# Sums of weights of four recurrent pairs formed in DRAM by adding DMAs on GpSimd's queue

## The chip, the cores and the metric

The kernel runs on one core of one Trainium2 chip. The core has five engines with a queue of instructions each: TensorE (PE in the profile, with its weight loads as PEld), VectorE (DVE), ScalarE (ACT), GpSimd (POOL) and SyncE (SP, which here only issues DMAs). Each engine takes its instructions in the order in which they were written into its queue; a semaphore that an instruction waits for holds up everything behind it on the same engine. The metric is the device time of one execution in microseconds.

## What is computed

One layer of a decoder: a normalised input goes through a combined projection into dilated attention heads and gated recurrent heads, then through an output projection and a gated convolution mixer. Only the recurrent part of the projection is touched by the change. Cut to that:

```python
u = rms_norm(h, norm1_g[layer])                       # h: 1024 tokens x 1024
proj = u @ w_in[layer]
aq, ak, av, hq, hf, hi, hg = jnp.split(proj, IN_SPLITS, axis=-1)
...
rec = hgrn2_mixer(hq.reshape(B, S, HGRN_HEADS, HGRN_FDIM),
                  hf.reshape(B, S, HGRN_HEADS, HGRN_FDIM),
                  hi.reshape(B, S, HGRN_HEADS, HGRN_IDIM), lb)
rec = rms_norm(rec, hgrn_norm_g[layer].reshape(HGRN_HEADS, HGRN_IDIM))
rec = rec * jax.nn.silu(hg.astype(jnp.float32).reshape(B, S, HGRN_HEADS, HGRN_IDIM))
```

`hq`, `hf` and `hg` have four heads of 128 columns each, so twelve blocks of weights, 1024 x 128.

## The kernel before

**Products.** Every float32 product is made of three TensorE products of rounded parts: an operand is split into a high part (`hi`, a copy in a narrower format, made on ACT, line 88) and the rest (`lo`, a subtraction on DVE, line 90). Lines 492 to 494 are those three products, 128x128 by 128x512 each.

**Seven products for eight.** Two blocks of weights are taken as a pair, whose four quarters of 128x512 are called a11, a12 (first block) and a21, a22 (second block). The pair is multiplied with the input by a Strassen-like scheme with seven products (`pair_block`). It needs, beside the four quarters, four sums: s1 = a21+a22, s3 = a21+a11, s2 = s1+a11, s4 = a12+s2. Class `PairMix` loads the four quarters into five staging buffers (`raww`) and makes the sums in place on DVE, one addition of 128x512 each (lines 164 to 166 and 183).

**The ring.** `Ring` holds a plan, a list of all weight tiles in the order in which they are used. For each it takes a staging buffer, has SP load 256 KB into it (line 68, or 300 and 155 for other layouts), splits it, and keeps five splits ahead of TensorE. A staging buffer is loaded anew when the subtraction on line 90 has read the tile that was in it.

**Order in time.** First come two passes over the input in eight steps each: the attention's values (`V`, written to DRAM tensor `vd`) and the recurrence's values (`I`, written to `ivd`). During `V`, the squares of the input are summed for the first norm: ACT squares a piece (line 444), POOL adds it to `sums0` or `sums1`, one for each half of the tokens (line 446). Between `V` and `I`, `rms1` multiplies these sums with a column of ones on TensorE (tile `sst`, line 452), and ACT and DVE make the tokens' scales from it. After that come the attention's projections (`qk`), the attention with one recurrent pair beside it (`HG[0]`), then four more pairs (`HG[1]` to `HG[4]`, the subject of the change) with the recurrence woven in (`dense`, `hg_block`), the last pair without the scheme, the output projection, and the mixer.

**What sets the order.** TensorE's order is the order of the program text. On the other engines a scheduler places instructions by its own estimate of when their inputs are there; only what is passed through `pin` keeps the order of the text. The squares' sums on POOL are pinned among themselves. Tiles in DRAM come from the pool `drv`.

**On POOL** there is little: the fourteen sums of squares until 47 us, then, from 77 us on, fills and scalings for the attention's mask (`far_t`, `tri`, `vec`, `sel`, lines 666 to 676) and later one scaling for each attention score tile (line 718).

The lines around which the seam between `V` and `I` turns:

```python
    ring.step = 1
    ring.fill(2)
    for hf in range(2):
        square_x(hf, NCT - 1, NCT - 1)
    ...
    rms1()
```

Of the kernel before, what the change touches and what calls it, by code (L numbers as in the profile page):

```python
# [10 lines left out]
F32 = mybir.dt.float32  # L11
# [3 lines left out]
ALU = mybir.AluOpType  # L15
PSUM = bass.MemoryType.PSUM

P = 128
# [3 lines left out]
H2 = 512  # L22
# [228 lines left out]
def hybrid_kernel(ctx: ExitStack, tc: tile.TileContext, xT, w_qk, w_tok, w_hg, w_out, w_up,  # L251
                  w_down, vecs, amask, hmask, out):
    nc = tc.nc
    PE, DVE, ACT, POOL = nc.tensor, nc.vector, nc.scalar, nc.gpsimd
# [32 lines left out]
    plan = []  # L287

    ORDER = ("a11", "s2", "a12", "s3", "s1", "a22", "s4")

    def want_mix(key, a, b, heads):
        m = PairMix(nc, a, b, heads)
        plan.extend(((key, x), getattr(m, x)) for x in ORDER)

    def tok(m, kh, c):

        def load(ring):
# [6 lines left out]
    HG = [(("hf", 0), ("hq", 0)), (("hg", 0), ("hg", 1)), (("hf", 1), ("hq", 1)), (("hf", 2), ("hq", 2)),  # L304
          (("hg", 2), ("hg", 3)), (("hf", 3), ("hq", 3))]
    def w_of(kind, h):
        return w_hg[4 * {"hq": 0, "hf": 1, "hg": 2}[kind] + h]
# [3 lines left out]
    for p in range(4):  # L311
        want_mix(("qk", p), w_qk[2 * p], w_qk[2 * p + 1], True)
    want_mix(HG[0], w_of("hf", 0), w_of("hq", 0), False)
    for pair in HG[1:-1]:
        want_mix(pair, w_of(*pair[0]), w_of(*pair[1]), False)
    plan.extend(((key, x), w_of(*key)[:, x * H2 : (x + 1) * H2]) for key in HG[-1] for x in range(2))

    OUT_BLOCKS = [[(hf, 0, d) for d in range(NCT) for hf in range(2) if d < SHARED or hf == 0], [(0, 1, d) for d in range(NCT)],
# [12 lines left out]
    for f in range(NFF):  # L331
        if f < 2:
            plan += [((x, f), part(f, i)) for x, i in (("a11", 0), ("a12", 3), ("a21", 1), ("a22", 2))]
        else:
            m = Mix(nc, w_up[f])
# [3 lines left out]
    ring = Ring(nc, ringp, plan)  # L339
# [56 lines left out]
    drv = drv_cm.__enter__()  # L396
# [12 lines left out]
    def vtile(name):  # L409
        return at.tile([P, H2], F32, tag="vi", name=name, bufs=4)  # L410
# [50 lines left out]
    def split_sum(x, c, src):  # L461
        hi, lo = (y[:, c] for y in opn[x])
        pin(ACT.copy(hi, src))
        pin(DVE.tensor_sub(lo, src, f32(hi)))

    def sums_a(c):
        x11, x12 = xt[0, c], xt[1, c]
        g = col(V_G1 + c)
        pin(DVE.tensor_sub(x11, x12, x11))
        pin(ACT.mul(x11, x11, g))  # L470
        pin(ACT.mul(x12, x12, g))

    def sums_b(c):

        x11, x21, x12, x22 = xt[0, c], xt[0, KS + c], xt[1, c], xt[1, KS + c]
        g2 = col(V_G1 + KS + c)

        def less(x, src, y):
            pin(DVE.scalar_tensor_tensor(x, src, g2, y, op0=ALU.mult, op1=ALU.subtract))

        split_sum("T1", c, x11)
        less(x12, x22, x12)
        less(x22, x22, x11)
        less(x21, x21, x22)
        split_sum("T2", c, x22)
        split_sum("T3", c, x12)

    def sums_c(c):
        split_sum("T4", c, xt[0, KS + c])
# [49 lines left out]
    def tok_step(key, c, banks, order):  # L539

        w = ring.get((key, c))
        for t in order:
            bh, bl = opn[OPS1[2 * (t // KS) + c // KS]]
            tk = slice((t % KS) * P, (t % KS + 1) * P)
            three(banks[t], (bh[:, c % KS, tk], bl[:, c % KS, tk]), w, c == 0, c == NCT - 1)
        ring.done((key, c))
# [12 lines left out]
    def tok_out(dst, t, x, src):  # L559
        if src is x or t % 2:  # L560
            DVE.tensor_scalar(x, src, R1T[:, t : t + 1], 1.0, op0=ALU.mult, op1=ALU.mult)
        else:
            ACT.mul(x, src, R1T[:, t : t + 1])
        nc.scalar.dma_start(dst[t * P : (t + 1) * P], x)

    fill = Fill()

    ring.order = ring.pin = pin
# [33 lines left out]
    for c in range(NCT):  # L602
        tok_step("I", c, V, range(NCT) if c < 4 else TURN)
        if c < 2:
            sums_a(2 + c)
        if c < 3:
            sums_b(1 + c)
        if c == 0:
            for t in range(NCT):
                tok_out(vd, t, vt[t], vt[t])  # L610
        if 4 <= c:
            sums_c(c - 4)
    ring.order = ring.pin = lambda ins: ins
    ring.step = 99
    for t in TURN:
        x = vtile(f"it{t}")
# [201 lines left out]
    with pool("hg", "right") as hg:  # L818
# [8 lines left out]
        def tile_of(kind, h, hf):  # L827
            tag, bufs = {"hf": ("A", 4), "hq": ("E", 5), "hg": ("GH"[h // 2], 4)}[kind]
            return ht(tag, f"{tag}{h}_{hf}", bufs)
# [108 lines left out]
        for hf in range(2):  # L938
            for kind, h in HG[0]:
                x = tile_of(kind, h, hf)  # L940
# [693 lines left out]
```

## Time and profile before

| | us |
|---|---|
| median of 3 runs | 1147.45 |
| lowest and highest of them | 1146.85, 1148.58 |
| the profiled execution, its time | 1148.54 |
| its span in the trace | 1146.7 |
| TensorE busy | 1133.0 |
| VectorE busy | 959.9 |
| ScalarE busy | 587.0 |
| GpSimd busy | 87.7 |

The 1.8 us between the profiled execution's time and its span lie outside of the first and last traced instruction. Busy time counts an instruction from its start to its modelled end. On TensorE consecutive products overlap: a 128x512 product is listed with 0.39 us, while the next one starts 0.23 us after it; so a short wait of TensorE can hide within its busy time, and starts have to be compared. Line numbers are those of the kernel before; in the changed kernel the same lines stand 7 to 24 further down.

### The profile page before, as it was taken

The numbers are of one execution on the slowest core, as the hardware profiler recorded it, in microseconds if no ns is written. First come the engines' busy times: TensorE is split into PE (matmuls) and PEld (weight loads), VectorE is DVE, ScalarE is ACT, GpSimd is POOL, SyncE is SP. The second block draws the span as 40 slices with busy tenths as digits, with TensorE's granted clock in tenths as the row PEclk, the third lists the DMA queues.
The fourth block names the chain that finished last, engine by engine and source line by source line (L and its number), as shares of the span: only waits on it lengthen the run. The fifth ranks groups of instructions, "written<-read, shape, count | busy, mean of one in ns | idle before, by whom it ended". The sixth has DMA issues, their size and how long they took to land.

```text
span 1146.7 us, 17921 instructions
## 1 busy us (share of the span) xinstructions
PE 1133.0 (99%) x6412; PEld 929.9 (81%) x6412; DVE 959.9 (84%) x1748; ACT 587.0 (51%) x1177; POOL 87.7 (8%) x107
## 2 busy tenths in 40 slices
PE   9999999999999999999999999999999999999996
PEld 7887777778888888878788888888888888888885
DVE  7685877778999975889999989888988789857987
ACT  6444445465788875555434434343434344444553
POOL 5200233330000002000000000000000000000000
PEclk9999999999999999999999999999999999999998
DMA  7135222224313542321233233322332377435532
GB/s 250 49 108 152 57 73 65 85 75 159 110 57 110 169 134 94 92 65 46 70 114 113 89 102 129 111 78 97 128 111 83 116 262 230 118 101 175 156 114 80
DMA packets 98633, 129.84 MB, mean 113 GB/s; under 512 B 25008, under 2 KB 44240, under 8 KB 98544
## 3 DMA queue, kind: packets, MB, share of 16 engines
q1 hardware_dynamic: 84256, 104.03, 29.5%
q10 hardware_dynamic: 14288, 24.67, 5.8%
q8 instruction: 50, 0.82, 0.3%
q14 instruction: 39, 0.32, 0.1%
HBM read 97.58 MB, written 31.09 MB: 112 GB/s over the span
## 4 chain that ended last, share of the span: by engine, by line
PE 91%; DVE 7%; issue 1%; ACT 1%; DMA 1%; ACTq 0%; DVEq 0%; SPq 0%
PE p L1235 11%; PE p L1233 11%; PE p L1234 11%; PE w L492 5%; PE w L494 5%; PE w L493 5%; PE ds L1533 3%; PE ds L1534 3%; PE ds L1532 3%; PE da L1533 2%; PE da L1534 2%; PE da L1532 2%; PE po L492 2%; PE po L494 2%; PE po L493 2%; PE S L705 2%
## 5 line engine op out<-in xcount | busy, mean ns | idle before, releaser
L88 ACT CAST whi<-raww 128x512 fp32r<-128x512 f32 x257 | 157.6, 618 | 219.1 <-PE p L1234 75.2
L90 DVE TENSOR_TENSOR wlo<-raww,whi 128x512 fp32r<-128x512 f32 x258 | 179.9, 699 | 30.5 <-ACT whi L88 28.6
L88 ACT CAST whi<-r 128x512 fp32r<-128x512 f32 x70 | 43.6, 623 | 83.4 <-PE ds L1533 47.8
L90 DVE TENSOR_TENSOR wlo<-r,whi 128x512 fp32r<-128x512 f32 x70 | 48.0, 687 | 19.1 <-ACT whi L88 18.4
L1532 PE MATMUL ds<-fhi,whi 128*128 128x512 f32 x160 | 62.3, 389 | 0.0
L1534 PE MATMUL ds<-fhi,wlo 128*128 128x512 f32 x160 | 62.2, 389 | 0.0
L1233 PE MATMUL p<-b1h,whi 128*128 128x512 f32 x160 | 62.2, 389 | 0.0
L1234 PE MATMUL p<-b1l,whi 128*128 128x512 f32 x160 | 62.2, 389 | 0.0
L1235 PE MATMUL p<-b1h,wlo 128*128 128x512 f32 x160 | 62.2, 389 | 0.0
L1533 PE MATMUL ds<-flo,whi 128*128 128x512 f32 x160 | 62.2, 389 | 0.0
L718 POOL TENSOR_SCALAR P<-P,st 128x128 f32<-128x128 f32 (+7 forms) x64 | 46.4, 731 | 101.8 <-DVE st L717 96.6
L1506 POOL TENSOR_TENSOR facc<-facc,sqf 128x256 f32<-128x256 f32 x2 | 1.5, 736 | 673.8 <-ACT sqf L1505 673.8
L90 DVE TENSOR_TENSOR flo<-rawf,fhi 128x512 fp32r<-128x512 f32 x70 | 48.0, 686 | 3.9 <-ACT fhi L88 3.9
L88 ACT CAST fhi<-rawf 128x512 fp32r<-128x512 f32 x70 | 43.1, 616 | 14.6 <-PE p L1235 5.0
L716 ACT ACTIVATE P<-P,st 128x128 f32<-128x128 f32 (+7 forms) x64 | 35.7, 559 | 27.5 <-DVE st L714 27.5
L1262 ACT ACTIVATE cv<-cv 128x512 f32<-128x512 f32 x44 | 27.8, 633 | 40.3 <-DVE cv L1255 40.3
L1255 DVE SCALAR_TENSOR_TENSOR cv<-g,vec,cv 128x511 f32<-128x511 f32 (+2 forms) x92 | 44.7, 491 | 3.6 <-ACT cv L1252 3.3
L1532 PE MATMUL da<-fhi,whi 128*128 128x512 f32 x120 | 46.7, 389 | 0.0
L1533 PE MATMUL da<-flo,whi 128*128 128x512 f32 x120 | 46.7, 389 | 0.0
L1534 PE MATMUL da<-fhi,wlo 128*128 128x512 f32 x120 | 46.7, 389 | 0.0
L714 DVE CUSTOM_DVE_ANT_0 P<-S,mask 128x128 f32<-128x128 f32 (+7 forms) x64 | 28.9, 487 | 8.7 <-PE S L707 7.5
L1532 PEld LDWEIGHTS ds<-fhi,whi 128*128 128x128 f32 x160 | 30.0, 188 | 6.3
(622 smaller groups left out, 3408.7 us busy)
## 6 DMA issues: line engine op xcount, KB each, us to landing
raww<-in_w_up_dram SPq DMA_DIRECT2D x88, 256.0 KB, 2.9
rawf<-spT SPq DMA_DIRECT2D x40, 256.0 KB, 2.7
r<-in_w_down_dram SPq DMA_DIRECT2D x40, 256.0 KB, 3.3
spB<-a ACTq DMA_DIRECT2D x30, 256.0 KB, 2.2
spT<-t ACTq DMA_DIRECT2D x30, 256.0 KB, 2.1
rawf<-spB SPq DMA_DIRECT2D x30, 256.0 KB, 2.7
raww<-in_w_out_dram SPq DMA_DIRECT2D x28, 256.0 KB, 2.8
raww<-in_w_hg_dram SPq DMA_DIRECT2D x24, 256.0 KB, 2.6
```

The source lines that it names most:

```text
L88: self.pin(self.high(hi[:, :w], raw))
L90: self.pin(low.tensor_sub(lo[:, :w], raw, f32(hi[:, :w])))
L492: PE.matmul(ps, a[0], b[0], start=start, stop=False)
L493: PE.matmul(ps, a[0], b[1], start=False, stop=False)
L494: PE.matmul(ps, a[1], b[0], start=False, stop=stop)
L718: POOL.tensor_scalar(Pt[:, :n], Pt[:, :n], st[:, 3:4], 1.0, op0=ALU.mult, op1=ALU.mult)
L1233: PE.matmul(ps, hi[:, s], bhi, start=(start and n == 0), stop=False)
L1234: PE.matmul(ps, hi[:, s], blo, start=False, stop=False)
L1235: PE.matmul(ps, lo[:, s], bhi, start=False, stop=(stop and n == len(rhs) - 1))
L1532: PE.matmul(ps[d], hi[:, s], ahi, start=(k == 0), stop=False)
L1533: PE.matmul(ps[d], hi[:, s], alo, start=False, stop=False)
L1534: PE.matmul(ps[d], lo[:, s], ahi, start=False, stop=(k == NPAIR - 1))
```

## The change

```diff
+    wsum = {}
+
+    def quad(pair, x):
+        m, i = {"a11": (0, 0), "a12": (0, 1), "a21": (1, 0), "a22": (1, 1)}[x]
+        return w_of(*pair[m])[:, i * H2 : (i + 1) * H2]
+
     for pair in HG[1:-1]:
-        want_mix(pair, w_of(*pair[0]), w_of(*pair[1]), False)
+        plan.extend(((pair, x), quad(pair, x) if x[0] == "a" else lambda ring, pair=pair, x=x: ring.raw(wsum[pair, x]))
+                    for x in ORDER)
...
+    SUMS = (("s1", "a21", "a22"), ("s3", "a21", "a11"), ("s2", "a22", "s3"), ("s4", "a12", "s2"))
+
+    def sum_begin(pair):
+        for x, a, _ in SUMS:
+            wsum[pair, x] = drv.tile([P, H2], F32, name=f"ws{pair[0][0]}{pair[0][1]}_{x}")
+            nc.sync.dma_start(wsum[pair, x], quad(pair, a))
+
+    def sum_add(pair, i):
+        x, _, b = SUMS[i]
+        POOL.dma_start(wsum[pair, x], quad(pair, b) if b[0] == "a" else wsum[pair, b], accum_op=ALU.add, max_dma_last_dim=2048)
...
         if 4 <= c:
             sums_c(c - 4)
+        if c < len(HG) - 2:
+            sum_begin(HG[1 + c])
+        elif c > 4:
+            for i in (0, 1) if c == 5 else (2,) if c == 6 else (3,):
+                for pair in HG[1:-1]:
+                    sum_add(pair, i)
```

For each of the four pairs, four tiles of 128x512 in DRAM (`ws...`) first receive a copy of one quarter, by a DMA on SP's queue, and then a second quarter or an earlier sum, by a DMA on POOL's queue that adds to what is there. s2 waits for s3, and s4 for s2. In the text the copies stand in the steps 0 to 3 of `I`, the additions in its steps 5 to 7; neither is pinned. Later the ring loads all seven tiles of a pair as plain tiles; `PairMix` is left with the attention's pairs and `HG[0]`. So 16 DVE additions go, and 16 copies, 16 adding DMAs and 12 more loads of the ring (28 for 16) come.

TensorE's list of instructions is the same, row for row. On POOL this is the order around the last sums of squares (names: `sq0_6` is the square of piece 6 of the first half of the tokens; `DMASW` are the semaphores of POOL's own DMAs, `DMAHW` those of SP's and ACT's). Before:

```order
L446 TENSOR_TENSOR sums1_233<-sums1_233,sq1_5_442 128x512 [waits Activation_49]
L446 TENSOR_TENSOR sums0_231<-sums0_231,sq0_6_484 128x512 [waits Activation_49]
L446 TENSOR_TENSOR sums1_233<-sums1_233,sq1_6_487 128x512 [waits Activation_49]
L446 TENSOR_TENSOR sums0_231<-sums0_231,sq0_7_514 128x512 [waits Activation_49]
L446 TENSOR_TENSOR sums1_233<-sums1_233,sq1_7_517 128x512 [waits Activation_49]
L673 MEMSET far_t_1112 32x1024 [waits DVE_49,Pool_49]
```

And in the changed kernel, from the first sum of piece 6 to the last of piece 7:

```order
L453 TENSOR_TENSOR sums0_231<-sums0_231,sq0_6_484 128x512 [waits Activation_49]
L453 TENSOR_TENSOR sums1_233<-sums1_233,sq1_6_487 128x512 [waits Activation_49]
L582 DMA wshg0_s2_622<-wshg0_s3_620 128x512 [waits DMAHW6_49,DMASW1_49]
L582 DMA wshf1_s1_668<-in_w_hg_dram 128x512 [waits DMAHW1_49]
L582 DMA wshf1_s3_670<-in_w_hg_dram 128x512 [waits DMAHW2_49]
L582 DMA wshg0_s4_624<-wshg0_s2_622 128x512 [waits DMAHW7_49,DMASW2_49]
L582 DMA wshf1_s2_672<-wshf1_s3_670 128x512 [waits DMAHW3_49,DMASW4_49]
L582 DMA wshf2_s1_715<-in_w_hg_dram 128x512 [waits DMAHW6_49]
L582 DMA wshf2_s3_717<-in_w_hg_dram 128x512 [waits DMAHW7_49,DMASW0_49]
L453 TENSOR_TENSOR sums0_231<-sums0_231,sq0_7_514 128x512 [waits Activation_49]
L582 DMA wshf1_s4_674<-wshf1_s2_672 128x512 [waits DMAHW4_49,DMASW6_49]
L453 TENSOR_TENSOR sums1_233<-sums1_233,sq1_7_517 128x512 [waits Activation_49]
```

Two more additions (s1 and s3 of the pair hg0) stand ahead of piece 6, six behind the last sum and ahead of the fill of `far_t`. So the scheduler has moved ten of the sixteen ahead of the end of the pass `V`, and eight of them stand between the sums of piece 6 and the second sum of piece 7, which TensorE's product on line 452 reads.

On DVE, these rows stand in the first of the four pairs, just after the attention has ended (`G` are that pair's outputs, `w...` the banks of its products, `lb` small vectors of the recurrence, `wlo` the splits of the ring). Before:

```order
L90 TENSOR_TENSOR wlo56_3321<-raww43_2933,whi56_3320 128x512
L164 TENSOR_TENSOR raww49_3384<-raww47_3360,raww48_3362 128x512
L927 TENSOR_TENSOR lb_m_3280<-vec_63 128x4
L165 TENSOR_TENSOR raww47_3360<-raww46_3358,raww47_3360 128x512
L928 TENSOR_TENSOR lb_e_3281<-vec_63,lb_m_3280 128x4
L929 TENSOR_TENSOR lb_e_3281<-vec_63,lb_m_3280 128x4
L522 TENSOR_TENSOR G0_1_3325<-G0_0_3306,w37_3326 128x512
```

In the changed kernel:

```order
L90 TENSOR_TENSOR wlo56_3369<-raww46_3366,whi56_3368 128x512 [waits DMAHW4_49,PE_49,Activation_49]
L951 TENSOR_TENSOR lb_m_3326<-vec_63 128x4
L952 TENSOR_TENSOR lb_e_3327<-vec_63,lb_m_3326 128x4 [waits DVE_49]
L953 TENSOR_TENSOR lb_e_3327<-vec_63,lb_m_3326 128x4
L955 TENSOR_TENSOR lb_m_3326<-lb_e_3327 128x4 [waits Activation_49]
L956 RECIPROCAL lb_m_3326<-lb_m_3326 128x4 [waits DVE_49]
L957 TENSOR_TENSOR lb_67<-lb_e_3327,lb_m_3326 128x4 [waits DVE_49]
```

The two additions in place (`raww` from `raww`) are gone, and the small vectors follow the split at once.

## Prediction

> **What bounds the kernel now.** I read the busy times first, then the waits of the busiest engine, then the two stretches that the change touches.
>
> ```profile
> PE 1133.0 (99%) x6412; PEld 929.9 (81%) x6412; DVE 959.9 (84%) x1748; ACT 587.0 (51%) x1177; POOL 87.7 (8%) x107
> PE warm L420 <- DVE eps L281: 1.1, 1, 1.1
> PE w L492 <- ACT u L520: 1.0, 1, 1.0
> PE w L492 <- DVE G L530: 0.9, 1, 0.9
> PE p0g L1233 <- DVE h L1128: 0.8, 1, 0.8
> PE v L492 <- DVE whi L88: 0.3, 1, 0.3
> PE p L1235 <- DVE wlo L90: 0.2, 1, 0.2
> ```
>
> The first line is the page's: TensorE is busy for 99% of the span. The other six are the whole list of TensorE's waits (total, times, longest): 4.3 us altogether. Its list of instructions is the same in both kernels, so the change can win only from these waits and from waits too short to be listed. And whatever makes TensorE wait longer somewhere is paid in full, since no later wait is long enough to swallow it.
>
> ```profile
> 260.00:285.50 25.50, 24.64 (x162) 20.41 (x161) 21.63 (x45) 15.79 (x31) 0.00 (x0) 1.00 0.55 179
> 285.50:440.00 154.50, 154.50 (x851) 128.50 (x852) 140.49 (x253) 121.37 (x312) 3.97 (x4) 1.00 0.38 115
> ```
>
> These two stretches (start and end, length, then busy time of PE, PEld, DVE, ACT, POOL, granted clock, DMA share, GB/s) hold the four pairs. DVE is at 91% in the second, yet TensorE has no gap there. DVE's load is high but covered: TensorE sets the pace.
>
> **What goes: 16 additions on DVE.**
>
> ```profile
> L165 DVE TENSOR_TENSOR raww<-raww,raww 128x512 f32<-128x512 f32 x4 | 2.9, 726 | 0.0
> L164 DVE TENSOR_TENSOR raww<-raww,raww 128x512 f32<-128x512 f32 x4 | 2.8, 689 | 0.1
> L166 DVE TENSOR_TENSOR raww<-raww,raww 128x512 f32<-128x512 f32 x4 | 2.7, 680 | 0.0
> L183 DVE TENSOR_TENSOR raww<-raww,raww 128x512 f32<-128x512 f32 x4 | 2.7, 680 | 0.0
> 272.23 0.69 DVE L164 TENSOR_TENSOR raww<-raww,raww 128x512 f32<-128x512 f32 x1
> 276.52 0.69 DVE L523 TENSOR_TENSOR G<-w,G 128x512 f32<-128x512 f32 x1 [0.73 <-PE w L494]
> 278.40 0.68 DVE L166 TENSOR_TENSOR raww<-raww,raww 128x512 f32<-128x512 f32 x1
> 284.68 0.68 DVE L530 TENSOR_TENSOR G<-G,w 128x512 f32<-128x512 f32 x1
> 285.50 0.47 PE L492 MATMUL w<-B22h,whi 128*128 128x512 f32 x1 [0.86 <-DVE G L530]
> ```
>
> DVE loses 2.9 + 2.8 + 2.7 + 2.7 = 11.1 us. On TensorE's path only one place counts. At 285.50 it has waited 0.86 us for DVE's evacuation on line 530. DVE was last idle ahead of 276.52, for 0.73 us, and has been busy almost without a gap since. One removed addition lies in that stretch (278.40, 0.68 us); one like that of 272.23 lies ahead of the idle time, which has swallowed it. Without the addition in the stretch the evacuation comes 0.7 us earlier, and since the order there shifts more than one row, I count the whole wait: **0.9 us won** (0.86), with 0 as the other end if the recurrence's work on DVE moves into the place. Behind it nothing else is late: the 154.5 us after it show no gap. Of waits too short to be listed I count nothing in the sum.
>
> **What is added and hidden.** The 16 copies stand on SP between the loads of `I`.
>
> ```profile
> 23.34 1.79 DVE L90 TENSOR_TENSOR wlo<-raww,whi 128x512 fp32r<-128x512 f32 x1
> 28.46 1.77 DVE L90 TENSOR_TENSOR wlo<-raww,whi 128x512 fp32r<-128x512 f32 x1
> 34.08 0.69 DVE L90 TENSOR_TENSOR wlo<-raww,whi 128x512 fp32r<-128x512 f32 x1 [1.91 <-ACT whi L88]
> 3.62 0.44 SPq L431 DMA_DIRECT2D xs_kp<-in_xT_dram  x1
> SPq L300 <- DVE wlo L90: 36.0, 7, 10.4
> 28.70:51.56 22.86, 22.86 (x104) 18.93 (x102) 14.54 (x19) 11.57 (x20) 6.84 (x5) 1.00 0.15 47
> raww<-in_w_hg_dram SPq DMA_DIRECT2D x24, 256.0 KB, 2.6
> spT<-t ACTq DMA_DIRECT2D x30, 256.0 KB, 2.1
> x<-in_xT_dram SPq DMA_DIRECT2D x8, 256.0 KB, 5.6
> ```
>
> SP issues a DMA in 0.44 us, so 16 copies take 7 us of SP. SP has 36.0 us in which it waits for a staging buffer in seven of these loads, each released by a subtraction (the first three rows, which end at 25.13, 30.23 and 34.77 us). The copies of one pair follow each release. The DMA engines are 15% busy then. No copy from DRAM to DRAM is in this trace; its landing lies between a store's 2.1 us and the 5.6 us of the loads in the crowded first microseconds. Even with 5.6 us the four copies of the second pair have landed at 30.23 + 4 x 0.44 + 5.6 = 37.6 us, before POOL asks for them (38.97, below). So copies cost nothing; were the cover gone, a late weight tile would hold TensorE by up to one landing, 5.6 us at most. The 12 more loads of the ring (12 x 2.6 = 31 us if none overlapped another) come where the DMA engines are used for 0.55 and 0.38 of the time (the two stretches above), and a staging buffer that no longer holds a quarter for three sums comes free sooner; were that cover gone, each late tile would cost up to 2.6 us. What they read has landed long before.
>
> **What is added and not hidden.** It is POOL's queue at the end of the pass `V`.
>
> ```profile
> 35.89 3.08 POOL L446 TENSOR_TENSOR sums<-sums,sq 128x512 f32<-128x512 f32 x2 [6.20 <-ACT sq L444]
> 44.70 2.77 POOL L446 TENSOR_TENSOR sums<-sums,sq 128x512 f32<-128x512 f32 x2 [5.73 <-ACT sq L444]
> 77.18 0.95 POOL L673 MEMSET far_t<- 32x1024 f32 x1 [29.71 <-DVE T4l L464]
> 44.00 1.15 ACT L444 ACTIVATE sq<-x 128x512 f32<-128x512 f32 x2
> 51.40 1.84 PE L452 MATMUL sst<-ones,sums 128*128 128x1 f32 x16
> L446 POOL TENSOR_TENSOR sums<-sums,sq x14: 1286/1740/1752, 13.0 to 46.2; 128x512 f32<-128x512 f32 x14
> ```
>
> Now the last two sums end at 44.70 + 2.77 = 47.47 us, and TensorE needs them at 51.40: slack 3.9 us. In the changed kernel seven adding DMAs stand ahead of the first of these two sums and one more between them, after the sums of piece 6, which end at 35.89 + 3.08 = 38.97 us (the two DMAs ahead of these fall into POOL's 6.2 idle microseconds). Let c be how long one such DMA holds POOL, and w the time from there to its landing. From 38.97: three DMAs are issued (3c). The fourth, hg0_s4, waits for the landing of the first and runs within the next wait: the fifth, hf1_s2, adds hf1_s3, which was issued third, so it begins at 3c + w and ends at 4c + w. Two more (6c + w), one sum (1.39 us, half of 2.77), hf1_s4 (its input landed at 4c + 2w, earlier for w below 2c + 1.39), the last sum (1.39): the sums are ready at **38.97 + 7c + w + 2.78**.
>
> The trace has no DMA on this queue, so both are bounded by rows. c: from SP's issue, 0.44 us, to POOL's own pass over a tile of this size, median 1.74 us. w: from a store's 2.1 us less 0.4 of issue, 1.7 us, to 5.6 less 0.4, 5.2 us. With the low ends the formula gives 46.5, less than the 45.15 + 2.78 = 47.9 at which the squares (ACT's row at 44.00) let the sums be ready, and TensorE doesn't wait. With the high ends hf1_s4 is held by its input (4c + 2w = 17.4), and the end is 38.97 + 17.4 + 1.74 + 1.39 = 59.5: a wait of 8.1 us. I take c = 1.4, as a loop of POOL's program over 128 rows, nearest to its fastest passes (2.77 / 2), and w = 2.6, as a load of the same size: 38.97 + 9.8 + 2.6 + 2.78 = 54.15, a **wait of 2.75 us** at 51.40. All that TensorE has behind it (the steps of `I`) moves with it, and DVE's and ACT's scales with that.
>
> The Trainium skill (DMA: Bandwidth & Descriptors, section "Anatomy of one DMA — SWDGE (gpsimd) path") fits a DMA of this queue with 2.0 us plus its bytes at 436 GB/s, from issue to semaphore, 2.6 us for 256 KB. By it, and with c as taken, w would be 1.2 us, the wait 1.35 us and the result 1147.9 us, an estimate from that page; no run here shows such a DMA yet, and the fit is for plain loads, not for one that reads two operands.
>
> The six DMAs behind the last sum hold POOL for 6c and two landings at most, 6 x 1.4 + 2 x 2.6 = 13.6 us, until 67.8 us; `far_t` is due at 77.18. That is covered by 9 us.
>
> **The sum.** Against the profiled execution: 1148.54 + 2.75 - 0.86 = 1150.4 us (its span 1146.7 and the 1.8 around it). That execution is 1.1 us over the median of the three runs, 1147.45, so for the median I predict 1147.45 + 1.9 = **1149.3 us**.
>
> **The rivals.**
>
> *Hidden.* If c is at most (51.40 - 38.97 - 2.6 - 2.78) / 7 = 1.0 us, TensorE never waits and only the gain stays: 1146.6 us. For it speaks the 0.44 us issue on SP; against it that POOL builds the transfers by program.
>
> *A long queue on POOL (slower).* From c = 1.46 us on the wait is over 3.2 us and the loss over 2.3 us. With c = 1.74 and w = 2.6 the sums are ready at 56.53, a wait of 5.1 us. A wait of that length could also slow TensorE's clock, as in the start:
>
> ```profile
> 7.45 0.63 PE L493 MATMUL v<-wlo,B11h 128*128 128x512 f32 x1
> 7.88 0.63 PE L494 MATMUL v<-whi,B11l 128*128 128x512 f32 x1
> 10.36 0.40 PE L494 MATMUL v<-whi,B11l 128*128 128x512 f32 x1
> 11.05 0.39 PE L494 MATMUL v<-whi,T4l 128*128 128x512 f32 x1
> 11.27 0.39 PE L492 MATMUL v<-whi,T4h 128*128 128x512 f32 x1
> ```
>
> There products start 0.43 us apart until about 10.4 us, and 0.23 us apart from then on; twelve products at 0.2 us more are 2.4 us. The listed waits of 1.0 us brought no such stretch. So this rival gives 1147.45 + 5.1 + 2.4 - 0.9 = 1154.1 us, or 1151.7 without the slow clock. The Trainium skill (TensorE: Matmul & The Clock Gate, section "Part 1: The HAM clock gate") states that TensorE falls to half its clock after an idle window of about 3.4 us and needs about as long to come back; the first microseconds here agree in kind, and no wait of that length is in the trace.
>
> *DVE was the limit after all (faster).* If the 11.1 us taken from DVE also free TensorE's short unlisted waits:
>
> ```profile
> L492 PE MATMUL w<-T3h,whi 128*128 128x512 f32 x16 | 7.1, 447 | 0.0
> L493 PE MATMUL w<-T3l,whi 128*128 128x512 f32 x16 | 6.2, 389 | 0.0
> ```
>
> The first group of a product is 58 ns longer than the following, 0.9 us for 16, and this is the worst of seven such groups; all seven are under 7 x 0.9 = 6.5 us, and most of that is the change of banks, not DVE. Half of it with POOL's queue hidden would be 1147.45 - 0.9 - 3.2 = 1143.4 us.
>
> **How the numbers follow.** A short wait as forecast (c from 1.0 to 1.46): 0.41, with 1146.6 to 1149.8 us of its own. Hidden: 0.15. A long queue: 0.39. Faster through DVE: 0.05. About 0.2%, 2.3 us, is what can be told from no change here; so faster 0.05, same 0.41 + 0.15 = 0.56, slower 0.39. The range goes from the hidden case, less half of the runs' spread of 1.7 us, 1145.7, to the upper bounds of c and w: 1147.45 + 8.1 + 2.4 - 0.9 = 1157.0.
>
> **What would show it.** Right: POOL's adding DMAs follow one another from 39 us on at about 1.4 us each, the second last sum ends after 51.4, TensorE's list of waits has `sst` behind POOL with 1 to 3 us, and `w` behind `G` on line 530 is gone. Wrong: no wait at `sst` (c too large), one over 3.2 us (c or w too small), a product spacing of 0.43 us behind it (the slow clock), or a new wait of TensorE in the four pairs (the loads, or DVE's new order).

## The result and the profile after

| | median us | runs | lowest to highest |
|---|---|---|---|
| before | 1148.01 | 4 | 1146.85 to 1148.65 |
| after | 1161.97 | 4 | 1161.56 to 1163.76 |

The ratio of after to before is 1.0127, with a 95% interval of [1.0114, 1.0140]. The forecast was 1149.3 us with a range up to 1157.0: the time is outside of it, on the slow side. The profiled execution of the changed kernel took 1162.03 us, with a span of 1160.2.

The page of the changed kernel: busy time, share of the span, instructions; the last line is POOL's own DMA queue (packets, MB, share of sixteen DMA engines).

```profile
PE 1135.6 (98%) x6412; PEld 930.8 (80%) x6412; DVE 951.9 (82%) x1732; ACT 587.6 (51%) x1177; POOL 100.1 (9%) x123
q0 software_dynamic: 2304, 4.20, 2.3%
```

TensorE's waits in the changed kernel (total, times, longest):

```profile
PE sst L459 <- POOL sums L453: 8.7, 2, 7.3
...
PE w L499 <- ACT A L527: 0.9, 1, 0.9
PE w L499 <- DVE E L533: 0.8, 1, 0.8
PE w L499 <- DVE G L533: 0.8, 1, 0.8
```

DVE has lost its 16 additions. TensorE has a new wait of 8.7 us at `sst`, and in the four pairs it has three waits of 0.8 to 0.9 us where it had one.

TensorE's list of instructions is the same in both kernels, so the same instruction can be looked up in both traces. Its start, in us:

| instruction of TensorE | before | after | difference |
|---|---|---|---|
| a product of `V` in the start (`v<-whi,B11l`) | 10.36 | 8.78 | -1.6 |
| first product at `sst` | 51.40 | 57.23 | +5.8 |
| first product of `I` with `T4h` | 55.95 | 66.88 | +10.9 |
| a product of the first of the four pairs (`w<-T4h,whi`) | 281.76 | 293.67 | +11.9 |
| one of the second pair (`w<-T4h,whi`) | 304.70 | 317.16 | +12.5 |
| one of the third (`w<-B21h,whi`) | 319.47 | 332.99 | +13.5 |
| end of the span | 1146.7 | 1160.2 | +13.5 |

The loss is made in two places: 12.5 us between the end of `V` and the first steps of `I`, and 2.6 us in the four pairs. (The 1.6 us won in the start belong to this execution, not to the change: the same first products stand 0.23 us apart from 7.0 us on, and before only from 10.4 us on.)

POOL's timeline in the changed kernel (start, time, instruction, and in brackets the idle time before it with its releaser):

```profile
36.48 3.08 POOL L453 TENSOR_TENSOR sums<-sums,sq 128x512 f32<-128x512 f32 x2 [3.54 <-ACT sq L451]
41.18 0.81 POOL L582 DMA_DIRECT2D wshg_s<-wshg_s  x1 [1.63 <-DMA wshg_s<-in_w_hg_dram]
41.73 1.94 POOL L582 DMA_DIRECT2D wshf_s<-in_w_hg_dram  x2
50.49 0.80 POOL L582 DMA_DIRECT2D wshg_s<-wshg_s  x1 [6.83 <-DMA wshg_s<-wshg_s]
53.40 0.81 POOL L582 DMA_DIRECT2D wshf_s<-wshf_s  x1 [2.10 <-DMA wshf_s<-in_w_hg_dram]
53.92 1.97 POOL L582 DMA_DIRECT2D wshf_s<-in_w_hg_dram  x2
54.99 2.19 POOL L453 TENSOR_TENSOR sums<-sums,sq 128x512 f32<-128x512 f32 x1
58.42 0.81 POOL L582 DMA_DIRECT2D wshf_s<-wshf_s  x1 [1.24 <-DMA wshf_s<-wshf_s]
58.99 1.53 POOL L453 TENSOR_TENSOR sums<-sums,sq 128x512 f32<-128x512 f32 x1
```

The first row has the sums of piece 6, the seventh and the last have those of piece 7 that `sst` needs. Between them POOL hardly works: it waits for the copy or the adding DMA before (1.63), for one adding DMA (6.83), for a second (2.10) and for a third (1.24), 1.63 + 6.83 + 2.10 + 1.24 = 11.8 us in all. The last sum ends at 58.99 + 1.53 = 60.52 us; before, it ended at 47.47. The hold of POOL itself is short, 0.81 us for a DMA and some 0.5 us from one to the next (41.18 to 41.73).

The DMA issues of the changed kernel (instructions, KB each, median us from issue to landing):

```profile
wshg_s<-in_w_hg_dram SPq DMA_DIRECT2D x8, 256.0 KB, 5.0
wshf_s<-in_w_hg_dram SPq DMA_DIRECT2D x8, 256.0 KB, 7.7
wshg_s<-in_w_hg_dram POOLq DMA_DIRECT2D x4, 256.0 KB, 7.1
wshg_s<-wshg_s POOLq DMA_DIRECT2D x4, 256.0 KB, 6.4
wshf_s<-in_w_hg_dram POOLq DMA_DIRECT2D x4, 256.0 KB, 8.1
wshf_s<-wshf_s POOLq DMA_DIRECT2D x4, 256.0 KB, 5.9
```

And stretches of the changed kernel (start and end, length, busy time and instructions of PE, PEld, DVE, ACT, POOL, then granted clock, DMA share, GB/s):

```profile
36.00:42.00 6.00, 6.00 (x28) 4.99 (x27) 4.05 (x6) 2.76 (x5) 3.89 (x4) 1.00 1.05 326
54.00:60.00 6.00, 1.86 (x8) 1.78 (x8) 0.00 (x0) 0.00 (x0) 4.76 (x6) 0.50 1.02 171
```

Two things stand there. The DMA engines are full (1.05 by this view's count), where before they were used for 0.15 of the time; the DMAs of POOL's queue land after 6 to 8 us (medians) in that crowd. And the granted clock is 0.50 from 54 us on (0.50 from 60 to 66 us too): the long wait has cost TensorE its clock too. Its timeline in the changed kernel shows the price:

```profile
49.58 0.39 PE L501 MATMUL v<-whi,B22l 128*128 128x512 f32 x1
57.23 1.86 PE L459 MATMUL sst<-ones,sums 128*128 128x1 f32 x8 [7.27 <-POOL sums L453]
60.57 1.87 PE L459 MATMUL sst<-ones,sums 128*128 128x1 f32 x8 [1.47 <-POOL sums L453]
63.30 0.63 PE L501 MATMUL i<-whi,B11l 128*128 128x512 f32 x1
63.72 0.63 PE L499 MATMUL i<-whi,B11h 128*128 128x512 f32 x1
66.18 0.40 PE L499 MATMUL i<-whi,B11h 128*128 128x512 f32 x1
```

The sixteen products at `sst` took 3.73 us, twice the 1.84 of before, and the first products of `I` start 0.42 us apart (63.30 to 63.72) until the product at 66.18 is back at 0.40 us. The 12.5 us lost at the seam split at the start of the second eight products at `sst`. It comes 60.57 - 49.58 = 11.0 us after the last product of `V`; before, it came 1.0 us after it (51.17 to 52.2, the middle of the sixteen). These 9.9 us go to POOL's late sums, whatever the clock, since the first eight products are done before the second sum is there. The other 2.6 us come behind 60.57 and go with the low clock.

### The profile page after: what moved, and what is told of

Same layout as the page of the kernel before. It is cut to its first block, busy times and chain, and to the rows that moved or that the text cites. A ratio compares the mean times of both kernels' runs of the same rounds, so it can differ in the third digit from the quotient of the medians.

```text
span 1160.2 us, 17994 instructions
## 1 busy us (share of the span) xinstructions
PE 1135.6 (98%) x6412; PEld 930.8 (80%) x6412; DVE 951.9 (82%) x1732; ACT 587.6 (51%) x1177; POOL 100.1 (9%) x123
## 3 DMA queue, kind: packets, MB, share of 16 engines
q0 software_dynamic: 2304, 4.20, 2.3%
## 4 chain that ended last, share of the span: by engine, by line
PE 83%; DVE 8%; DMA 4%; ACT 2%; issue 2%; SPq 0%; POOL 0%; DVEq 0%; ACTq 0%
PE p L1259 11%; PE p L1257 11%; PE p L1258 11%; PE w L499 5%; PE w L500 4%; PE w L501 4%; PE ds L1557 3%; PE ds L1558 3%; PE ds L1556 3%; PE da L1557 2%; PE da L1558 2%; PE da L1556 2%; PE po L499 2%; PE po L501 2%; PE po L500 2%
```

## The experiments

Ratios are to runs of the kernel before on the same chip, whose median was 1146.9 us in all of them. These runs range from 1146.47 to 1149.22 us, so a median of few runs, like the 1148.01 of four above, can lie 1 us beside it without any change.

**1. The adding DMAs behind the last sums.** The DMAs are pinned, so that POOL runs them in the order of the text, behind the two sums of piece 7.

```diff
-        POOL.dma_start(wsum[pair, x], quad(pair, b) if b[0] == "a" else wsum[pair, b], accum_op=ALU.add, max_dma_last_dim=2048)
+        pin(POOL.dma_start(wsum[pair, x], quad(pair, b) if b[0] == "a" else wsum[pair, b], accum_op=ALU.add, max_dma_last_dim=2048))
```

> All sixteen adding DMAs are kept in text order behind the last sum of squares on POOL; the rest is the changed kernel. Theory A (POOL's queue: what stands ahead of the last sums makes TensorE wait, and the full DMA engines as such cost nothing): no wait at sst, no slow products after it, so of the changed kernel's shift 9.9 + 2.6 us go and the 2.7 us in the four pairs stay: 1148.0 + 2.7 = 1150.7 us, within 1.5. Theory B (the traffic itself: weights and the values' stores come late because the DMA engines are full): sst no longer waits, but TensorE waits for weight tiles or banks in the pass I instead, over 3 us of it: 1154 us or more.

Measured: 1149.55 us (1148.74 to 1152.16), ratio 1.0022 [1.0013, 1.0032]. Its windows, DMA issues and waits of TensorE:

```profile
30.00:36.00 6.00, 6.00 (x28) 4.99 (x27) 4.09 (x6) 2.88 (x5) 0.60 (x1) 1.00 0.85 263
36.00:42.00 6.00, 6.00 (x29) 4.95 (x28) 4.08 (x5) 3.09 (x6) 3.08 (x2) 1.00 0.92 300
66.00:72.00 6.00, 6.00 (x28) 4.96 (x27) 5.13 (x8) 2.96 (x6) 2.44 (x3) 1.00 1.10 289
```

```profile
vd<-vt ACTq DMA_DIRECT2D x8, 256.0 KB, 11.2
wshg_s<-in_w_hg_dram POOLq DMA_DIRECT2D x4, 256.0 KB, 10.6
```

```profile
PE w L499 <- ACT A L527: 0.9, 1, 0.9
PE w L499 <- DVE E L533: 0.8, 1, 0.8
PE w L499 <- DVE G L533: 0.6, 1, 0.6
```

The wait at `sst` is gone and the clock stays whole; most of the loss, 1.05 of the 1.27%, was where the scheduler had put the adding DMAs. The DMA work itself is all still there, and in a worse crowd: in 66 to 72 us the engines are full, and the stores of `vd` take 11.2 us, yet TensorE is busy throughout. In 30 to 42 us only the 16 copies and the kernel's own loads run, and these already fill the engines to 0.85 and 0.92. So the copies cost TensorE nothing directly. They are a part of the crowd in which the adding DMAs land late, and the adding DMAs are the other: the last copy is issued at 46.4 us, and from 54 to 84 us the share is 1.04 to 1.16. No run has the copies alone. What is left, 0.22%, goes with the three waits in the pairs.

**2. TensorE kept busy in the wait.** Ahead of the products at `sst`, 60 products whose results nobody reads; the rest is the changed kernel.

```diff
         st = bank("o", "sst")
+        for _ in range(60):
+            PE.matmul(st[:, 128:512], opn["B11"][0][:, 0, 0:P], opn["B11"][0][:, 0, 0:384], start=True, stop=True)
```

> The changed kernel with 60 products of 128x384 written to unused columns of the bank of sst, ahead of it; they fill TensorE's wait and compute nothing that is read. If the slow products after the wait come from the clock that fell during it: spacing 0.23 us from the first product of I on, granted clock 1.00, and 2.6 us won: 1159.4 us. If they come from the full DMA engines or from late operands: spacing stays at 0.43 us and the time at 1162.0 us.

Measured: 1159.52 us (1158.63 to 1161.29), ratio 1.0107 [1.0092, 1.0122]. TensorE's timeline in this kernel:

```profile
49.52 10.59 PE L458 MATMUL sst<-B11h 128*128 128x384 f32 x60
59.95 1.84 PE L461 MATMUL sst<-ones,sums 128*128 128x1 f32 x16
61.97 0.39 PE L502 MATMUL i<-wlo,B11h 128*128 128x512 f32 x1
62.19 0.39 PE L503 MATMUL i<-whi,B11l 128*128 128x512 f32 x1
```

The sums come as late as before, but the sixteen products take 1.84 us again and the products of `I` are 0.22 us apart from the start. Adding work to TensorE made the kernel faster by the difference of the ratios, 1.0127 - 1.0107 = 0.20%, 2.3 us, near the 2.6 us read from the trace. (The two intervals overlap a little, but the slowest run here, 1161.29 us, is faster than the fastest of the changed kernel, 1161.56.)

**3. No work in DRAM at all.** The copies and adding DMAs are left out, and the ring loads plain quarters in place of the sums, so the sums aren't formed. The ring's loads and DVE's work are those of the changed kernel.

```diff
-        plan.extend(((pair, x), quad(pair, x) if x[0] == "a" else lambda ring, pair=pair, x=x: ring.raw(wsum[pair, x]))
+        plan.extend(((pair, x), quad(pair, x if x[0] == "a" else {"s1": "a21", "s3": "a21", "s2": "a22", "s4": "a12"}[x]))
                     for x in ORDER)
```

> No copies and no adding DMAs; the ring loads seven plain tiles of each of the four pairs, but quarters in the place of the four sums, so the sums are left out of the computation. The stage of the four pairs is as in the changed kernel, the passes V and I as before. If the 2.7 us lost in that stage come from the scheduler's new order on DVE and ACT: they stay, 1150.7 us. If they come from tiles read from DRAM sums, or from what the crowd left behind: they go, and the wait of 0.9 us before it too: 1147.1 us.

Measured: 1149.83 us (1149.05 to 1151.59), ratio 1.0023 [1.0013, 1.0032], the same as with the adding DMAs behind the sums, with the same waits on `A`, `E` and `G` (0.9, 0.8, 0.7 us). So the loss in the four pairs doesn't come from the work in DRAM. It comes from what is left: 12 more loads and 16 fewer additions, and the order that the scheduler makes of it. (Experiment 6 has the same loads and additions, and separates the order from them.)

**4. Plain copies in place of the adding ones.** Same DMAs, same queue, same waits, without `accum_op=ALU.add`; the sums are not formed.

> The changed kernel with plain copies in the place of the adding DMAs, on the same queue with the same waits, so the sums are not formed. If adding makes those DMAs slow (two operands read, then written): landing falls from 6 to 8 us to 4 us or less, the wait at sst from 8.7 us to 2 us or less, the time to about 1153 us. If the crowd of copies makes them slow: landing stays over 5 us, the wait over 6 us, the time over 1159 us.

Measured: 1156.51 us (two runs), ratio 1.0079 [1.0058, 1.0099]. The page's queue line, two rows of the DMA issues and TensorE's timeline at `sst` in this kernel:

```profile
q0 software_dynamic: 1280, 4.20, 1.2%
```

```profile
wshg_s<-in_w_hg_dram POOLq DMA_DIRECT2D x4, 256.0 KB, 4.8
wshf_s<-in_w_hg_dram POOLq DMA_DIRECT2D x4, 256.0 KB, 6.0
```

```profile
51.13 1.05 PE L459 MATMUL sst<-ones,sums 128*128 128x1 f32 x8 [1.38 <-POOL sums L453]
55.03 1.87 PE L459 MATMUL sst<-ones,sums 128*128 128x1 f32 x8 [2.85 <-POOL sums L453]
```

The same 4.20 MB take 1280 packets instead of 2304, and 1.2% of the sixteen engines' span instead of 2.3%: adding costs the DMA engines about twice a copy (2.3% of 1160.2 us over 16 DMAs is 1.7 us of all engines for each, against 0.9). Landings are some 2 us shorter, and the two waits at `sst` come to 1.38 + 2.85 = 4.2 us, half of 8.7. So the place in POOL's queue costs a wait without any addition in it, and the adding makes it about twice as long. Neither of my two cases came out alone: the time lies between the 1153 of the one and the 1159 of the other, and landings are 4.3 to 6.0 us. The clock fell here as well.

**5. One pair only.** The copies and adding DMAs are kept for the first of the four pairs, free to move as in the changed kernel; the other three pairs add on DVE as before.

```diff
     for pair in HG[1:-1]:
+        if pair is not HG[1]:
+            want_mix(pair, w_of(*pair[0]), w_of(*pair[1]), False)
+            continue
...
-        if c < len(HG) - 2:
-            sum_begin(HG[1 + c])
+        if c == 0:
+            sum_begin(HG[1])
...
-                for pair in HG[1:-1]:
-                    sum_add(pair, i)
+                sum_add(HG[1], i)
```

> Only the first of the four pairs has its sums made in DRAM (4 copies, 4 adding DMAs); the other three load four quarters each and add on VectorE as before. Theory (the landings of 6 to 9 us come from a crowd of 16 copies and 16 adding DMAs that fills the DMA engines): the DMA share in 36-54 us stays under 0.6, an adding DMA lands in 3 to 4.5 us after its issue instead of 5.9 to 8.1, the last sum of squares is not late, no wait at sst over 0.5 us, time 1146.9 within 0.8 of it. Rival A (an adding DMA takes 6 us or more by itself, full engines or not): landings of 6 us and more here too; the fourth adding DMA waits for the third in front of the last sums, 39.9 + 6 + 0.8 = 46.7, so even then sst waits under 1 us, and the rival is told by the landing, not by the time. Rival B (the hold on POOL is what delays): 0.81 us a hold here too, 4 holds, no wait.

Measured: 1148.41 us (1146.88 to 1150.07, 11 runs), ratio 1.0007 [0.9998, 1.0016]. POOL's timeline and two windows of this kernel:

```profile
39.59 0.81 POOL L585 DMA_DIRECT2D wshg_s<-wshg_s  x1
43.98 0.81 POOL L585 DMA_DIRECT2D wshg_s<-wshg_s  x1 [3.58 <-DMA wshg_s<-wshg_s]
45.38 2.77 POOL L456 TENSOR_TENSOR sums<-sums,sq 128x512 f32<-128x512 f32 x2 [0.58 <-ACT sq L454]
```

```profile
30.00:36.00 6.00, 6.00 (x28) 4.99 (x27) 4.09 (x6) 3.12 (x6) 2.24 (x3) 1.00 0.85 206
36.00:42.00 6.00, 6.00 (x28) 4.95 (x28) 4.05 (x6) 2.85 (x5) 3.83 (x3) 1.00 0.41 75
```

With the engines at 0.41 the third adding DMA released POOL after 4.4 us (39.59 to 43.98); the same DMA took 9.3 us in the changed kernel, at 1.05. The fourth stands ahead of the last sums here too, but these are ready in time, and no wait at `sst` is listed. My expectation of a share under 0.6 from 36 to 54 us held only just (0.41, 0.60, 0.16). Ahead of it, from 30 to 36 us, the share is 0.85 with one pair alone, and the two DMAs issued there landed after 6.1 us. Its DMA issues have both:

```profile
wshg_s<-in_w_hg_dram POOLq DMA_DIRECT2D x2, 256.0 KB, 6.1
wshg_s<-wshg_s POOLq DMA_DIRECT2D x2, 256.0 KB, 3.9
```

That goes with the crowd too, though two pairs of DMAs don't separate the crowd from being the first on the queue. The time missed my expectation of 1146.9 within 0.8; the interval of the ratio holds 1, the runs range as widely as those of the kernel before, and in the two profiles, of this run and of the kernel before, every product of TensorE starts within 0.2 us of the same time.

This run also tests the 0.9 us of the forecast by itself: the first pair has lost its additions on DVE, and TensorE waits in the same place for as long, now for a split on ACT:

```profile
285.34 0.47 PE L502 MATMUL w<-B22h,whi 128*128 128x512 f32 x1 [0.85 <-ACT whi L88]
```

**6. The evacuations first.** Experiment 1, and in addition the instructions that take the four pairs' products out of their banks (one copy on ACT and seven instructions on DVE for each pair) are given the scheduler's highest priority. **7. The same priority in the kernel before**, as a control.

```diff
+        def first(f, *a):
+            if dense:
+                with tc.high_priority():
+                    f(*a)
+            else:
+                f(*a)
...
-        ACT.copy(c1, (yield from step(1)))
+        first(ACT.copy, c1, (yield from step(1)))
...
-        DVE.tensor_sub(u, c1, (yield from step(6)))
+        first(DVE.tensor_sub, u, c1, (yield from step(6)))
```

> The kernel with the adding DMAs kept behind the last sums (1149.55, ratio 1.0022), and in addition the evacuations of the four pairs' products (the copy on ScalarE, the six additions and subtractions on VectorE) emitted at the scheduler's highest priority, so that they stand ahead of the recurrence's activations and of the ring's splits that are ready at the same time. Theory (the 2.5 us in the four pairs are waits of TensorE for evacuations that the new order puts behind other work on ScalarE and VectorE): the waits at 305, 308 and 321 us go, the copy stands ahead of four of the seven activations that it stood behind, time 1147.3 (1146.5 to 1148.2), ratio 0.9995 to 1.001. Rival (the loss there is DRAM traffic or the ring's loads arriving late): the waits stay or turn into waits on the ring's splits, 1149 or more.

> The kernel before with the same priority for the evacuations of the four pairs, as a control. Theory (only the new order has waits there that priority takes away; before, one of 0.86 us at 285 us): 1146.9 within 0.7; if the wait at 285 goes, 1146.0 and not below. Rival (evacuations ahead of everything is worth 2 us whatever the sums): 1145 or less, and then the 2 us that the other run gains say nothing about the order that the change brought.

Measured: experiment 6 1147.18 us (1145.50 to 1148.50), ratio 0.9995 [0.9987, 1.0004]; the control 1146.18 us (1145.57 to 1148.03), ratio 0.9989 [0.9980, 0.9997]. ACT's timeline in the kernel before, at the copy that frees a bank for the third pair:

```profile
317.19 0.58 ACT L520 COPY A<-w 128x512 f32<-128x512 f32 x1
```

In experiment 1:

```profile
317.75 0.63 ACT L800 ACTIVATE F<-F 128x512 f32<-128x512 f32 x1
...
320.36 0.62 ACT L802 ACTIVATE A<-A 128x512 f32<-128x512 f32 x1
320.88 0.56 ACT L527 COPY A<-w 128x512 f32<-128x512 f32 x1
```

And in experiment 6:

```profile
315.00 0.61 ACT L809 ACTIVATE A<-A 128x512 f32<-128x512 f32 x1
315.52 0.57 ACT L525 COPY A<-w 128x512 f32<-128x512 f32 x1
```

In the kernel before these activations of the recurrence (lines 776 to 778, from 318.53 on) stand behind the copy. In experiment 1 all six of them stand ahead of it, from 317.75 on, and TensorE waits 0.9 us for it; in experiment 6 one of them does, and the list of TensorE's waits has none in the four pairs. That gains 0.27% over experiment 1 (1.0022 - 0.9995; 2.4 us by the medians), against 0.11% (0.7 us) that the same priority brings to the kernel before. So the loss in the four pairs was the order on ACT and DVE: the loads are as many as in experiment 1, and the loss is gone. And with both losses mended, sums in DRAM and sums on DVE can't be told apart: the intervals of 6 and 7 overlap, and the control, which does all 16 additions on DVE, has the lower median.

## Why the prediction was wrong

Two terms of the sum failed: the landing w of an adding DMA, 2.6 us in the forecast and 8.5 measured, and the gain in the four pairs, 0.9 us in the forecast and a loss of 2.6 measured. The place and the kind of the wait at `sst` were right.

- **What bounds the kernel.** Right, and it is why the miss is large: TensorE's order is fixed, and every wait added was paid in full.
- **The 0.9 us won.** It did not come, and in experiment 5 the wait stayed as well, with only its releaser changed. In the changed kernel a wait of 0.8 us on `G` is still in the list, some 4 us earlier in TensorE's work. The bound I gave, 0 if the recurrence's work moves into the place, was too narrow on the other side: the new order also put waits on `E` and `A` into the next two pairs, and the four pairs became 2.6 us longer. The step that failed is counting a removed instruction as time won within a schedule that is made anew. The control (7) shows the other half: the same wait at 285 us goes without taking any addition away.
- **The copies.** That they cost TensorE nothing themselves was right (experiment 1). The reading behind it was wrong: 0.15 was the DMA share without them; with them it is 0.85 to 0.92, and with the adding DMAs 1.05. I used the old share for the new transfers.
- **The queue on POOL.** The mechanism, the place and the order of the rows were right. The term that was mis-sized is w, the landing: taken 2.6 us with bounds 1.7 to 5.2, measured 9.3 - 0.8 = 8.5 us for hg0_s2. The hold c was too large: 1.4 taken, 0.81 measured and 0.5 back to back, so these errors partly cancelled. With w so long, POOL also waited for its input in front of hf1_s4 (1.24 us), which the formula had as an aside for the high end only, and it waited 1.63 us ahead of the first DMA, which the formula put at nothing. With c = 0.81 and w = 8.5 this branch of the formula, 38.97 + 4c + 2w + c + 1.39, gives 61.4 us, near the 60.52 measured. With c = 0.81 and experiment 5's w of 4.4 - 0.8 = 3.6 us the same branch gives 38.97 + 3.24 + 7.2 + 0.81 + 1.39 = 51.6 us, a wait of 0.2: it is the landing that decides here, and the forecast weighed the hold. The Trainium skill (DMA: Bandwidth & Descriptors, section "Anatomy of one DMA — SWDGE (gpsimd) path") gave 2.6 us from issue to semaphore by its fit for plain loads; the rows here are 3.9 us at the quietest and 5.9 to 8.1 in the changed kernel, so the measurement decides against it for this kind of DMA.
- **Behind the last sum.** Covered as forecast, though later: the last adding DMA starts at 75.13 us rather than ending by 67.8, and no wait for `far_t` appears.
- **The rivals.** The long queue on POOL is what happened, with its slow clock (2.4 us forecast, 2.3 us shown by experiment 2) and 9.9 us lost to the late sums (8.7 of listed waits) against its upper bound of 8.1. I had put its own value at 5.1 us and 0.39 on it. The range's upper end, 1157.0, would have been 1147.45 + 9.9 + 2.6 + 2.6 = 1162.6 us with what the traces show for the sums, the clock and the four pairs: of the 5.6 us that it lacked, 3.5 are the last term, +2.6 in place of -0.9. DVE as the limit is excluded: taking its additions away brought nothing in experiments 1, 3 and 6. That rival's remark that the 58 ns of a first group are mostly the change of banks is not shown: in experiment 7 four products in a row start in another bank (277.11, 279.83, 282.55 and 285.27 us) with 0.39 us, as any other.

## What to carry to other kernels

A DMA that waits for another DMA stands in its engine's queue like any instruction: before it is put on an engine with other work, look at what the scheduler places behind it, and price the wait with the DMA share that the new transfers themselves make. Work taken off a covered engine brought nothing here, and where a scheduler makes the order anew it cost 0.22%; look at whether the instructions that free TensorE's banks still stand ahead of the others. Where a long wait of TensorE can't be removed, filling it can keep the clock: here that was worth 2.3 us.

## What the hardware showed that was not expected

- An adding DMA from DRAM to DRAM of 256 KB used about twice the DMA engines' time of a plain copy (2.3% and 1.2% of the span for 16), and held POOL for 0.81 us. Its landing went with the load of the engines: 3.9 us at a share of 0.41 to 0.60 (experiment 5, the median of two), 6 to 8 us at 1.05 (changed kernel), 10.6 us where eight of them were issued back to back (experiment 1).
- The full engines slowed the other queues with them: the stores of `vd` took 6.0 us in the changed kernel and 11.2 us in experiment 1, against 2.5 us in experiment 3, where there was no work in DRAM.
- TensorE's clock fell in experiment 4 too, where no single listed wait was longer than 2.85 us: the first eight products at `sst` took 1.05 us after a wait of 1.38, the second eight, after the 2.85, took 1.87. Small products between two waits didn't keep the clock. The Trainium skill (TensorE: Matmul & The Clock Gate, section "Part 1: The HAM clock gate") gives about 3.4 us for the idle window that lowers the clock; the wait of 7.3 us agrees, this row shows that a listed wait may be shorter.
- TensorE's first products came to full speed at 10.4 us before and at 7.0 us in the changed kernel, though both had their first product of `V` at 5.1 to 5.3 us; that was worth 1.6 us of the time. The same section of the Trainium skill says that the window runs freely and isn't started by the kernel, and that the point of change moves with it; the two traces agree in kind.
